# A macaron block with an RWKV mixer: the mixer's products put in a written order of twelve slots, its chunk states by a transition matrix, and w_out started beside the last group

## The chip, the cores and the metric

The kernel runs on one core of one Trainium2 chip. The metric is the device time of one execution in microseconds (us). The kernel before took 2170.04 us (median of 3 executions, 2164.2 to 2172.92). Engines are named as the profile does: PE is TensorE's matrix products, PEld its weight loads, DVE is VectorE, ACT is ScalarE, POOL is GpSimd, SP issues the DMAs of weights.

## The reference

One block on 256 rows of width 2048, float32. A vector `c` gives nine modulation vectors (`silu(c) @ w_ada + b_ada`); then three sublayers follow, each a norm, a modulation, a function, a second norm and a gated residual:

```
x = sandwich(x, ffn1)    swiglu, 2048 -> 5632 -> 2048
x = sandwich(x, mixer)   p = h @ w_in;  concat(pool(p[:512]), rwkv7(p[512:])) @ w_out
x = sandwich(x, ffn2)
```

The mixer's RWKV part has 24 heads of size 64. For every head a 64x64 state is carried over the 256 time steps:

```
state = state * w_t + (state @ -kk_t) (kk_t * a_t)^T + v_t k_t^T;   y_t = state @ r_t
```

after which each head's `y` is normed, gets a bonus `sum(r k r_k) v` and is gated by `sigmoid(xg) @ g2`. The pool part takes windowed means over time of four groups of 128 columns and multiplies each by a small matrix.

## The kernel before, in words

The kernel keeps float32 accuracy by splitting every operand of a large product into a rounded high part and a remainder (`split`, L182 on ACT makes `hi`, L183 on DVE makes `lo`), and multiplies hi·hi, hi·lo and lo·hi (`mm3`, L192 to L194; `rows_mm`, L526 to L528). Weights stream through `load` (L172) on the SP queue. The modulation vectors are no matrix products: `ada_step` loads rows of `w_ada` (L238, L241), DVE adds them up scaled by `silu(c)` (L245, L247), and small products sum over partitions (L254, L264). These steps are sprinkled over the three sublayers by counters; `ada_finish` forces what must be done by a given point.

The program is scheduled at build time: instructions are traced in the written order, which is their priority, and a scheduler with its own idea of durations fixes each engine's queue from priorities and readiness. `high_priority(n)` moves an instruction n places forward; `after` adds an edge that only fixes an order on one engine.

The mixer (`mixer`) goes in these parts:

- `outer`: the first group of w_in columns (the LoRA columns and r, k, v of the first four heads) while the normed input `hT` is made block by block.
- Six groups of four heads (two pairs of heads each, 256 columns). For each group after the first, three calls of `dense` make r, k, v (16 k-tiles, 2 column tiles and 3 products: 96 products of 128x256 each, 288 a group), and `tick` in `dense` gives out a piece of `w_ada` every third load (`ADA_MIXER = 3`).
- `stage(g, ...)` alternates two generators: `rwkv_a(g)` prepares group g, `rwkv_b(g-1)` runs the recurrence of the group before. The scheduler mixes them with the dense products.
- Then the pool columns (`dense` twice, `pool_branch`), the conversion of `y` to `hT` (L840, L841), and w_out in three column blocks (`rows_block`).

`rwkv_a`, for 4 chunks of 64 steps in each of two pairs of heads (U = 8 units of two heads): decay and gates from the LoRA products (L923, L926), their exponentials (L298); `L` (L942), the sum of squares `ns` (L944), the norm (`rsqrt`: L952, L298 twice, L309, L310, L311); `kk` (L957), `ar` (L965, L966), `kk*a` (L967), `bk` (L970 to L972); the products `G` of each chunk (L988, masked by L991); `T1` (L994); the bonus (L1003); then the inverse of a triangular 64x64 matrix per unit: 8x8 blocks on DVE (L1014 to L1030), two doublings with 32x32 products (L1054, L1062), a last one (L1075, L1082), which give `X`; the centred values `SV` (L1090) and transposes `bt` (L1097).

`rwkv_b` walks the four chunks in turn. Each chunk c > 0 needs: `ar` times the state (L1128), an addition to `rhs` on DVE (L1130), `X` times `rhs` (L1133), copies into `SV` on ACT and DVE (L1134, L1135), `bt` times `SV` plus the old state through the identity (L1144, L1141), a scaling on DVE (L1145). Then `y` (L1153, L1156), its variance (L1162), the norm (L1167, L1169), the gate (L1174) and the result (L1176).

PSUM has eight banks: two of tag `mm` for the dense products and six named `sa`, `ga`, `pb`, `zb`, `sb`, `y`. `raws` holds two weight tiles and two `ada` tiles, the split pool four pairs of `hi` and `lo`.

## Time and profile before

| what | value |
| --- | --- |
| median of 3 executions | 2170.04 us |
| the profiled execution: its own time, span of the trace | 2177.15 us, 2175.4 us |
| PE, DVE, ACT busy, share of the span | 95%, 74%, 47% |
| mean granted TensorE clock | 0.977 |
| first feed-forward sublayer | 0 to about 800 us |
| mixer, `outer` | about 805 to 876 us |
| mixer, six groups (first product of L923 to the pool products) | 876 to 1301 us |
| mixer, w_out | about 1301 to 1395 us |
| second feed-forward sublayer | 1395 us to the end |

In the rows below a busy PE is a union of records, and a record of a 128x256 product lasts 0.28 us, though the next one can start 0.12 us after it: idle time of PE is therefore what is left after the last record's whole length. A float32 product that isn't split (those of `rwkv_a` and `rwkv_b`) shows two records, a transpose one. PEclk is the granted clock as a share of full speed; in this trace it is either 1.0 or 0.5.

### The profile page before, as it was taken

What the parts mean: (1) busy time and instruction counts of PE and PEld (TensorE: products, weight loads), DVE (VectorE), ACT (ScalarE), POOL (GpSimd) and SP (SyncE); (2) the same over time, 40 slices, a digit from 0 to 9 for tenths busy, and PEclk for the clock granted to TensorE, in tenths of its full rate; (3) what the DMA queues carried; (4) which work ended last, traced back from release to release, by engine and by line L of the source; (5) the groups of instructions that cost most, each with busy time, mean ns of one, the idle gap of its engine ahead of it and who ended that gap; (6) DMA issues with size and microseconds to landing.
All of it is one profiled execution on the core that took longest, in us unless ns stands there. A gap on an engine that the chain in (4) does not pass through costs nothing.

```text
span 2175.4 us, 38002 instructions
## 1 busy us (share of the span) xinstructions
PE 2076.2 (95%) x15603; PEld 1838.6 (85%) x15603; DVE 1599.7 (74%) x2237; ACT 1016.9 (47%) x1497; POOL 0.2 (0%) x4
## 2 busy tenths in 40 slices
PE   4999999999999998989999989999999999999998
PEld 3999988888888887878887878799999888888886
DVE  6788898888887778766677565777989855555556
ACT  4534543444434465644534445653454344443443
POOL 0000000000000000000000000000000000000000
PEclk8999999999999999999999999999999999999999
DMA  9999888989888748634423315599887855555553
GB/s 324 347 317 321 280 288 314 335 308 320 312 320 297 253 127 256 179 86 139 124 67 103 102 60 194 205 346 318 280 302 266 295 193 188 182 192 194 194 184 126
DMA packets 313405, 502.37 MB, mean 231 GB/s; under 512 B 12966, under 2 KB 173839, under 8 KB 312975
## 3 DMA queue, kind: packets, MB, share of 16 engines
q1 hardware_dynamic: 311740, 496.59, 67.7%
q10 hardware_dynamic: 1490, 3.36, 0.5%
q8 instruction: 122, 2.00, 0.4%
q14 instruction: 53, 0.43, 0.1%
HBM read 497.77 MB, written 2.12 MB: 230 GB/s over the span
## 4 chain that ended last, share of the span: by engine, by line
PE 84%; DVE 8%; DMA 3%; ACT 2%; issue 2%; SPq 0%; DVEq 0%; ACTq 0%
PE mm L199 16%; PE mm L193 9%; PE mm L194 9%; PE mm L192 9%; PE mm L200 8%; PE mm L526 8%; PE mm L528 8%; PE mm L527 8%; DVE lo L183 2%; DMA ada<-in_w_ada_dram 1%; DVE acc L247 1%; DMA raw<-in_w_in_dram 1%; PE mm L254 1%; DVE G L991 1%; ACT hi L182 1%
## 5 line engine op out<-in xcount | busy, mean ns | idle before, releaser
L182 ACT CAST hi<-raw 128x1024 fp32r<-128x1024 f32 (+2 forms) x766 | 694.0, 913 | 862.8 <-PE mm L193 291.9
L183 DVE TENSOR_TENSOR lo<-raw,hi 128x1024 fp32r<-128x1024 f32 (+2 forms) x766 | 796.0, 1050 | 382.6 <-ACT hi L182 372.1
L199 PE MATMUL mm<-hT,hi 128*128 128x512 f32 x1536 | 540.1, 395 | 0.0
L192 PE MATMUL mm<-hT,hi 128*128 128x256 f32 x1824 | 525.3, 291 | 7.2 <-ACT hT L360 4.3
L193 PE MATMUL mm<-hT,hi 128*128 128x256 f32 x1824 | 527.4, 290 | 3.5 <-DVE hT L365 3.5
L194 PE MATMUL mm<-hT,lo 128*128 128x256 f32 x1824 | 525.0, 289 | 5.0 <-DVE lo L183 4.1
L200 PE MATMUL mm<-hT,lo 128*128 128x256 f32 x1536 | 431.9, 281 | 0.9 <-DVE lo L183 0.9
L247 DVE SCALAR_TENSOR_TENSOR acc<-ada,csilu,acc 128x1024 f32<-128x1024 f32 (+1 forms) x300 | 352.1, 1174 | 78.0 <-DMA ada<-in_w_ada_dram 75.4
L192 PEld LDWEIGHTS mm<-hT,hi 128*128 128x128 f32 x1824 | 353.5, 195 | 14.1 <-ACT hT L360 6.5
L193 PEld LDWEIGHTS mm<-hT,hi 128*128 128x128 f32 x1824 | 355.1, 195 | 9.4 <-DVE hT L365 5.4
L194 PEld LDWEIGHTS mm<-hT,lo 128*128 128x128 f32 x1824 | 354.3, 194 | 10.0 <-DVE lo L183 5.2
L199 PEld LDWEIGHTS mm<-hT,hi 128*128 128x128 f32 x1536 | 288.8, 188 | 67.8
L200 PEld LDWEIGHTS mm<-hT,lo 128*128 128x128 f32 x1536 | 288.0, 188 | 1.6 <-DVE lo L183 1.3
L526 PE MATMUL mm<-hi,act 128*128 128x512 f32 (+1 forms) x656 | 252.3, 385 | 0.0
L528 PE MATMUL mm<-hi,act 128*128 128x512 f32 (+1 forms) x656 | 251.9, 384 | 0.0
L527 PE MATMUL mm<-lo,act 128*128 128x512 f32 (+1 forms) x656 | 251.9, 384 | 0.0
L528 PEld LDWEIGHTS mm<-hi,act 128*128 128x128 f32 x656 | 123.3, 188 | 24.4
L526 PEld LDWEIGHTS mm<-hi,act 128*128 128x128 f32 x656 | 123.2, 188 | 24.3
L527 PEld LDWEIGHTS mm<-lo,act 128*128 128x128 f32 x656 | 123.3, 188 | 24.3
L609 DVE TENSOR_TENSOR act<-act,mm 128x512 f32<-128x512 f32 x96 | 64.2, 680 | 4.1 <-PE mm L194 3.8
L254 PE MATMUL mm<-ones,acc 128*128 128x1 f32 x128 | 20.0, 284 | 26.0 <-DVE acc L247 26.0
L254 PEld LDWEIGHTS mm<-ones,acc 128*128 128x128 f32 x128 | 20.0, 243 | 26.9 <-DVE acc L247 20.7
(382 smaller groups left out, 1794.3 us busy)
## 6 DMA issues: line engine op xcount, KB each, us to landing
raw<-in_ffn_w_down_dram SPq DMA_DIRECT2D x88, 1024.0 KB
raw<-in_ffn_w_gate_dram SPq DMA_DIRECT2D x86, 1024.0 KB
raw<-in_ffn_w_up_dram SPq DMA_DIRECT2D x86, 1024.0 KB
ada<-in_w_ada_dram SPq DMA_DIRECT2D x160, 512.0 KB
ada<-in_w_ada_dram SPq DMA_DIRECT2D x256, 256.0 KB
raw<-in_w_in_dram SPq DMA_DIRECT2D x34, 1024.0 KB
raw<-in_w_out_dram SPq DMA_DIRECT2D x16, 1024.0 KB
raw<-in_w_in_dram SPq DMA_DIRECT2D x9, 512.0 KB
```

What stands on the lines that cost most here:

```text
L182: a = nc.scalar.copy(hi, raw)
L183: d = nc.vector.tensor_tensor(lo, raw, hi.bitcast(F32), ALU.subtract)
L192: nc.tensor.matmul(ps, hi, x[:, 0, :], start=start, stop=False)
L193: nc.tensor.matmul(ps, hi, x[:, 1, :], start=False, stop=False)
L194: nc.tensor.matmul(ps, lo, x[:, 0, :], start=False, stop=stop)
L199: nc.tensor.matmul(ps.rearrange("p a t -> p (a t)"), hi, x.rearrange("p a t -> p (a t)"), start=start, stop=False)
L200: nc.tensor.matmul(ps[:, 0, :], lo, x[:, 0, :], start=False, stop=stop)
L247: self.later(nc.vector.scalar_tensor_tensor(acc, raw[:, i], ck, acc, ALU.mult, ALU.add))
L526: nc.tensor.matmul(ps, x[:, 0, ts], hi, start=start, stop=False)
L527: nc.tensor.matmul(ps, x[:, 0, ts], lo, start=False, stop=False)
L528: nc.tensor.matmul(ps, x[:, 1, ts], hi, start=False, stop=stop)
L609: nc.vector.tensor_tensor(part, part, bank, ALU.add)
```

## The change

Only the mixer's six groups, the start of w_out and the order of `w_ada` pieces change.

- **A written order on PE.** From the end of `outer` to the last recurrence, every product is tied behind the one written before it (`pe`, `mul`). A stage has 12 slots. A slot has two pieces of the next group's dense products (a piece is two k-tiles of one `dense`, 12 products), then the next segment of `b_old` (the recurrence two groups back), of `b` (one group back) and, in slots 0, 2, 4, 5, 6, 8 and 9, of `a`; after that a piece of `w_ada`. The other engines' queues are made by the scheduler as before.
- **Segments.** `rwkv_a` has seven: (0) LoRA products and exponentials, (2) `L`, `ns`, norm, `ar`, `bk`, (4) and (5) `G` of each pair, (6) transposes `bt` while DVE makes `T1` and the 8x8 blocks, (8) the product with `same` and the 8x8 inverse, (9) bonus and `SV`. `rwkv_b` has thirteen: the four 32x32 steps of the inverse, with `rhs` and the transposes `At` of `ar` beside them (0 to 3), the last doubling (4, 5), `X` times `rhs` and `X` times `At` = `Q` (6), the states of three chunks (7 to 9), `y` (10), variance and norm (11), and gate and result in slot 0 of the stage after (12).
- **One transition matrix per chunk.** `F = I + Q bt` and `E = ar + Q G` are made for all chunks at once in segment 7. Then a chunk's state is `bt SV + F S` in one PSUM tile and one scaling; the products of `ar` with the state, the addition to `rhs`, `X` times the corrected `rhs` and the identity products are gone from the walk over chunks. Per group 12 products (`ar` with the state) go, 44 come (`At` 12, `X At` 12, `Q bt` 8, `Q G` 12), and 8 are replaced one for one (`F S` for the identity).
- **Banks and tiles.** `rwkv_a` uses `sa` and `ga` alone, `rwkv_b` the other four. Some tiles lose or gain buffers, and four temporaries lie in parts of `yT` that are filled late.
- **Pool.** The pool columns are the dense pieces of the sixth stage (16 pieces, slots 0 to 7); the four `pool_branch` calls stand in its slots 8 to 11.
- **w_out.** A seventh stage holds the last recurrence, with two pieces (12 products of 128x512) of w_out's first column block per slot, taking k-tiles in the order 4 to 13, 0, 1; then 2, 3 and, last, 14 and 15, which come from the last group.
- **`w_ada`.** No pieces in `outer`; in the six stages 0.7 of a piece per slot (one load and one sum), until one more block, the third of five for the second feed-forward sublayer, is done before w_out.

```diff
-ADA_AHEAD = 1
-ADA_FFN1, ADA_MIXER, ADA_OUT, ADA_FFN2 = 2.8, 3, 3, 12
+ADA_AHEAD = ((7, 6), 2)
+ADA_FFN1, ADA_MIXER, ADA_OUT, ADA_FFN2 = 2.8, 0.7, 3, 12
+SLOTS, A_SLOTS = 12, (0, 2, 4, 5, 6, 8, 9)
...
+    def pe(self, op):
+        if self.ordered:
+            if self.pe_last is not None:
+                self.after(op, self.pe_last, "order")
+            self.pe_last = op
+        return op
+    def mul(self, ps, a, b, start=True, stop=True):
+        return self.pe(self.nc.tensor.matmul(ps, a, b, start=start, stop=stop))
...
+    def ada_run(self, upto):
+        while self.ada_pos < self.ada_end[upto]:
+            cols, k0 = self.ada_tasks[self.ada_pos]
+            width = cols[0][2]
+            per = 512 // width
+            if k0 == 0:
+                self.acc = self.tile(self.accs, [P, 2, width], tag="acc")
+            for kk in range(k0, k0 + 4, per):
+                raw = self.ada_load(cols, kk, per)
+                yield
+                self.ada_sum(raw, self.acc, kk, per)
+            self.ada_pos += 1
+            if k0 == KD - 4:
+                yield
+                self.ada_mod(cols, self.acc, self.bank("ga"))
...
     def dense(self, w, c0, n, x, cb):
...
             raw = self.load(w, 8 * kc, 8, c0, n * P)
-            self.tick()
...
                         self.mm3(ps[:, c, :], hi[:, k, cs], lo[:, k, cs], x[:, kt], kt == 0 and c == 0,
                                  kt == KD - 1 and c == n - 1)
+                yield
         for c in range(n):
             cb(c, ps[:, c, :])
...
+        for kc in order:
             raw = load(kc)
...
                         hi, lo = self.split(raw[:, pc:pc + per, 512 * h:512 * h + 512])
                         for b in (2 * h, 2 * h + 1):
                             use(b, k0, hi, lo)
+                        yield
                     continue
...
+        self.late = [self.yT[:, k:k + 2, :].rearrange("p k t -> p (k t)") for k in (0, 2, 12, 14)]
...
+        self.ordered = True
+        ada = self.ada_run(ADA_AHEAD)
+        slots = parts = 0
+        def stage(a, b, b_old, pieces, tasks):
+            nonlocal slots, parts
+            for s in range(SLOTS):
+                for _ in range(2):
+                    next(pieces, None)
+                for run, at in ((b_old, range(SLOTS)), (b, range(SLOTS)), (a, A_SLOTS)):
+                    if run and s in at:
+                        next(run, None)
+                if s in tasks:
+                    tasks[s]()
+                slots += 1
+                if a and int(slots * ADA_MIXER) > parts and (s not in A_SLOTS or s < A_SLOTS[-1]):
+                    parts += 1
+                    next(ada, None)
+        def weights(g):
+            for which in range(3):
+                self.split_ahead = 3000 if g == 1 and which < 1 else 300
+                yield from self.dense(w_in, POOL_WIDTH + which * R + g * 2 * P, 2, self.hT,
+                                      lambda i, ps: take(which, 2 * g + i, ps))
+        us = {}
+        def pool_weights():
+            for h in range(2):
+                yield from self.dense(w_in, h * 2 * P, 2, self.hT, lambda i, ps: us.__setitem__(2 * h + i, ps))
+        n = NP // 2
+        b = b_old = None
+        for g in range(n):
             state[g] = {}
-            stage(g, self.rwkv_a(state[g], g, *(rkv[g, w] for w in range(3)), lw))
-        self.pool_w = self.tile(self.w2p, [P, len(POOL_WINDOWS), P], tag="Wi", bufs=1)
-        nc.sync.dma_start(self.pool_w, I["pool_w"].rearrange("i p c -> p i c"))
-        stage(NP // 2)
-        for h in range(2):
-            self.dense(w_in, h * 2 * P, 2, self.hT, lambda i, ps: self.pool_branch(2 * h + i, ps))
-        for k in range(KD):
-            y = self.yT[:, k, :]
-            nc.scalar.copy(self.hT[:, k, 0, :], y)
-            nc.vector.tensor_tensor(self.hT[:, k, 1, :], y, self.hT[:, k, 0, :].bitcast(F32), ALU.subtract)
-        self.ada_finish((5,), self.mm)
+            a = self.rwkv_a(state[g], g, *(rkv[g, w] for w in range(3)))
+            pieces = weights(g + 1) if g < n - 1 else pool_weights()
+            tasks = {8 + i: partial(lambda i: self.pool_branch(i, us[i]), i) for i in range(4)} if g == n - 1 else {}
+            stage(a, b, b_old, pieces, tasks)
+            b, b_old = self.rwkv_b(g, state[g]), b
+            for run in (pieces, a):
+                for _ in run:
+                    pass
+        for _ in ada:
+            pass
...
+            order = [2, 3, 4, 5, 6, 0, 1, 7] if q == 0 else None
+            pieces = self.rows_pieces(load, KD, 1, lambda k: self.hT[:, k], banks, q == 3, done, more, self.mm, w, order)
+            if q == 0:
+                late(range(4, 12))
+                tasks = {1: lambda: late((12, 13)), 2: lambda: late(range(4))}
+                stage(None, b, b_old, pieces, tasks)
+                for _ in b:
+                    pass
+                late((14, 15))
+                self.ordered, self.pe_last = False, None
+            for _ in pieces:
+                pass
...
+        bt = self.tile(self.w2p, [P, U, P], tag="bt")
+        for h, tag in enumerate(("sa", "ga")):
+            ps = ch(self.bank(tag))
+            for u in range(U):
+                self.pe(nc.tensor.transpose(ps[:, u, :], pairs[h][u], self.ident[hs[h], hs[h]]))
+            nc.scalar.copy(bt[:, :, hs[h]], ps)
...
+        ps = self.bank("ga")
+        mul(ps, self.blocks, rk)
+        bv = self.tile(self.w2p, [P, 2 * T], tag="bv")
+        nc.vector.tensor_tensor(bv, ps, v, ALU.mult)
+        SV = self.tile(self.w2p, [P, U, 2, C], tag="SV")
+        ps = ch(self.bank("sa"))
+        for u in range(U):
+            for h in range(2):
+                mul(ps[hs[h], u], v[hs[h], u * C:(u + 1) * C], self.center[hs[h]])
+        for h in range(2):
+            nc.scalar.copy(SV[hs[h], :, h, :], ps[hs[h]])
+        st.update(G=G, ar=ar, bv=bv, T1=T1, Z0=Z0, Z1=Z1, SV=SV, bt=bt, wc=wc)
...
     def rwkv_b
...
+            if n == 0:
+                ps = ch(self.bank("zb"))
+                for u, h in units:
+                    mul(ps[hs[1 - h], u], G[hs[h], h, u, :C], SV[hs[h], u, h, :])
+                rhs = self.tile(self.w2p, [P, U, C], tag="rhs", bufs=1)
+                nc.scalar.copy(rhs, ps)
+            else:
+                ps = three(self.bank("y"))
+                for i, c, h in rest:
+                    mul(ps[hs[1 - h], i, c - 1], ar[hs[h], u_of(i, c), 0, :], self.ident[hs[h], hs[h]])
+                At = own("At")
+                nc.scalar.copy(At, ps)
...
+        ps, pq = ch(self.bank("pb")), three(self.bank("zb"))
         for u, h in units:
...
+            mul(ps[hs[1 - h], u], X[hs[1 - h], u], rhs[hs[1 - h], u])
+        for i, c, h in rest:
+            mul(pq[hs[1 - h], i, c - 1], X[hs[1 - h], u_of(i, c)], At[hs[1 - h], i, c - 1])
+        Q = own("Q")
+        nc.scalar.copy(SV[hs[0], :, 1, :], ps[hs[0]])
+        nc.vector.tensor_copy(SV[hs[1], :, 0, :], ps[hs[1]])
+        nc.scalar.copy(Q, pq)
         yield
...
+        E, F = own("At"), self.tile(self.w2p, [P, 2, NC - 2, C], tag="F", bufs=1)
+        for c in range(NC - 1):
+            for i, h in pairs:
+                u = u_of(i, c)
+                mul(sb[hs[h], c, i], bt[:, u, hs[h]], SV[:, u, h, :], i == 0, c == 0 and i == 1)
+            if c == 0:
+                pe, pf = three(self.bank("pb")), self.bank("zb")[:, :2 * (NC - 2) * C]
+                pf = pf.rearrange("p (i c t) -> p i c t", i=2, c=NC - 2)
+                for i, k, h in rest:
+                    q, u = hs[1 - h], u_of(i, k)
+                    if k < NC - 1:
+                        mul(pf[hs[h], i, k - 1], Q[q, i, k - 1], bt[q, u, hs[h]])
+                for i, k, h in rest:
+                    q, u = hs[1 - h], u_of(i, k)
+                    mul(pe[hs[h], i, k - 1], Q[q, i, k - 1], G[q, h, u, C:])
+                nc.vector.tensor_tensor(F, pf, self.eye.unsqueeze(1).unsqueeze(1).broadcast_to([P, 2, NC - 2, C]), ALU.add)
+            else:
+                for i, h in pairs:
+                    mul(sb[hs[h], c, i], F[hs[h], i, c - 1], S[hs[h], c - 1, i, :], False, i == 1)
+            nc.vector.tensor_tensor(S[:, c], sb[:, c], wc.rearrange("p (i c) o -> p i c o", i=2)[:, :, c, :]
+                                    .broadcast_to([P, 2, C]), ALU.mult)
+            if c == 0:
+                nc.vector.tensor_tensor(E, pe, ar.rearrange("p (i c) a t -> p i c a t", i=2)[:, :, 1:, 1, :], ALU.add)
             yield
...
         yp = self.bank("y")
         y = lambda c, i, h: half(yp, i)[hs[h], c * C:(c + 1) * C]
         for c in range(NC):
...
+            for i, h in pairs:
+                u = u_of(i, c)
+                mul(y(c, i, h), SV[:, u, h, :], G[:, h, u, C:], c == 0 and i == 0, False)
         for c in range(1, NC):
...
+            for i, h in pairs:
+                mul(y(c, i, h), S[hs[h], c - 1, i, :], E[hs[h], i, c - 1], False, c == NC - 1 and i == 1)
...
```

374 lines of the change are left out of this document (163 added, 211 removed).

## The prediction, made before the changed kernel ran

> **What bounds the kernel now.** The page comes first: the span, and PE busy for 95% of it. A busy PE says little about a single stretch, so next comes the view of busy time per engine by windows, cut at `outer` and at the first product of line 988 in each group of the mixer (the first row of groups starts at L923, the last ends with the pool). Columns: window, its length, busy us of PE, PEld, DVE, ACT, POOL, granted clock, DMA share, GB/s.
>
> ```profile
> span 2175.4 us, 38002 instructions
> PE 2076.2 (95%) x15603; PEld 1838.6 (85%) x15603; DVE 1599.7 (74%) x2237; ACT 1016.9 (47%) x1497; POOL 0.2 (0%) x4
> ```
>
> ```profile
> 805.00:875.80 70.80, 61.95 (x472) 57.06 (x471) 56.11 (x100) 44.50 (x89) 0.00 (x0) 0.98 0.83 235
> 875.80:952.00 76.20, 69.83 (x878) 61.47 (x878) 53.11 (x109) 44.18 (x83) 0.00 (x0) 0.96 0.48 140
> 952.00:1030.20 78.20, 70.23 (x936) 61.31 (x936) 56.93 (x118) 33.56 (x64) 0.00 (x0) 0.93 0.42 127
> 1030.20:1093.90 63.70, 61.49 (x892) 53.06 (x890) 45.34 (x98) 31.71 (x60) 0.00 (x0) 1.00 0.38 106
> 1093.90:1165.70 71.80, 68.59 (x918) 59.96 (x916) 46.46 (x102) 32.83 (x62) 0.00 (x0) 0.93 0.34 95
> 1165.70:1238.30 72.60, 68.61 (x912) 59.85 (x908) 46.36 (x99) 32.62 (x62) 0.00 (x0) 0.91 0.31 92
> 1238.30:1301.50 63.20, 56.07 (x855) 45.56 (x851) 47.33 (x127) 25.21 (x56) 0.00 (x0) 0.95 0.24 72
> ```
>
> The six groups take 425.7 us. PE is idle for 30.9 of them (length less busy, row by row), and the clock column costs 23.2 more (0.04 x 76.2 + 0.07 x 78.2 + 0.07 x 71.8 + 0.09 x 72.6 + 0.05 x 63.2). The one group at full clock takes 63.7 us, its neighbours 71.8 to 78.2. So PE's own work is most of each group, and the change can win from idle time and clock alone. The view of waits on PE in the same stretch says what ended the idle time (columns: us in total, times, longest), and two more windows show what follows one of these waits:
>
> ```profile
> PE ga L988 <- DVE bk L972: 3.0, 4, 0.8
> PE sa L886 <- DVE G L884: 2.9, 1, 2.9
> PE zb L1062 <- issue: 2.8, 2, 2.6
> PE sa L1003 <- DVE G L991: 2.6, 5, 0.8
> PE y L1117 <- issue: 2.0, 1, 2.0
> PE pb L1075 <- issue: 2.0, 2, 1.7
> ```
>
> ```profile
> 1121.00:1124.40 3.40, 2.50 (x48) 2.05 (x48) 1.93 (x4) 1.21 (x3) 0.00 (x0) 1.00 0.03 6
> 1124.40:1134.70 10.30, 10.30 (x53) 9.96 (x52) 1.65 (x5) 2.55 (x5) 0.00 (x0) 0.50 0.08 13
> ```
>
> No wait is long; some 45 are spread over the stretch, and since a 0.28 us record hides the first 0.16 of each, they cost about 7 us beyond the idle time. The largest kind is "issue": PE waits for nothing shown, in the middle of runs of 32x32 products. Idle time of 0.9 us in a window of 3.4 is enough to be followed by 10.3 us at half clock.
>
> The Trainium skill ("TensorE: Matmul & The Clock Gate", section "Why this matters for your kernels") asks only that idle gaps stay below about 3 us for the clock to hold. By it, no gap that I expect below would cost clock and the forecast would be 2140 us. The two rows differ from it: 0.9 us did.
>
> **The change, part by part.** Credit: all of the idle time, hidden waits and clock loss of the six groups, 30.9 + 7 + 23.2 = 61.1 us; then every loss of the new order is counted afresh. The prices of products are in the timeline of PE (start, length, records):
>
> ```profile
> 967.46 0.92 PE L1156 MATMUL y<-ar,S 64*64 64x64 f32 x24
> 972.77 0.75 PE L1062 MATMUL zb<-pm,Z 32*32 32x32 f32 x64
> 1088.19 0.28 PE L192 MATMUL mm<-hT,hi 128*128 128x256 f32 x1
> 1091.03 0.28 PE L192 MATMUL mm<-hT,hi 128*128 128x256 f32 x1
> 1093.67 0.45 PE L1128 MATMUL sb<-S,ar 64*64 64x64 f32 x8 [0.35 <-DVE S L1145]
> 1094.88 0.37 PE L988 MATMUL ga<-ar,bk 64*128 64x128 f32 x1 [0.75 <-DVE bk L972]
> ```
>
> *Products.* A 64x64 product costs 0.077 us in a long run (0.92 us for 12) and 0.11 in a burst of four (0.45). Per group 44 come in long runs (3.4 us) and the 12 of L1128 go (1.4): +2.0 us, 12 us for six groups. Bounds 2.0 to 4.0 each; I take the low end, since all four new kinds stand in runs of 8 or 12. The transposes, masks and copies that only move cost PE nothing new.
>
> *The walk over chunks.* Three hand-offs per chunk become one, with at least the slot's dense pieces between: 24 products at 0.118 us (24 starts from 1088.19 to 1091.03), 2.84 us. A link there is one or two DVE or ACT operations, so it fits; this was already hidden by dense products before and is no gain by itself.
>
> *`issue`.* The 32x32 runs now stand a slot apart. Their waits are in the credit; nothing is charged for them.
>
> *The wait that comes.* Segment 2 of `rwkv_a` (slot 2) ends with `ns`; segment 4 (slot 4) needs `ar` and `bk`. The chain of DVE and ACT between, in the timeline of the fourth group:
>
> ```profile
> 1083.78 0.69 DVE L952 TENSOR_SCALAR t<-ga 128x512 f32<-128x512 f32 x1 [0.84 <-PE ga L944]
> 1084.57 0.61 ACT L298 ACTIVATE t<-t 128x512 f32<-128x512 f32 x1
> 1085.58 0.62 ACT L298 ACTIVATE t<-t 128x512 f32<-128x512 f32 x1
> 1087.51 0.63 ACT L309 ACTIVATE t<-t 128x512 f32<-128x512 f32 x1
> 1088.17 0.69 DVE L310 SCALAR_TENSOR_TENSOR t<-t,t 128x512 f32<-128x512 f32 x1 [0.23 <-ACT t L309]
> 1089.38 0.68 DVE L311 SCALAR_TENSOR_TENSOR t<-t,t 128x512 f32<-128x512 f32 x1
> 1090.42 0.88 DVE L957 SCALAR_TENSOR_TENSOR kk<-k,cols,t 128x256 f32<-128x256 f32 x2
> 1091.62 0.69 DVE L965 TENSOR_TENSOR ar<-kk,W 128x512 f32<-128x512 f32 x1
> 1092.62 0.68 DVE L967 TENSOR_TENSOR kk<-kk,bk 128x512 f32<-128x512 f32 x1
> 1093.54 0.68 DVE L970 TENSOR_TENSOR bk<-t,Wi 128x512 f32<-128x512 f32 x1
> 1094.14 0.68 DVE L972 SCALAR_TENSOR_TENSOR bk<-kk,Wi 128x512 f32<-128x512 f32 x1
> ```
>
> It took 11.0 us here, among other work, and PE still waited 0.75 (the last row of the fence before). Its own operations sum to 7.5 us; hand-offs of 0.03 to 0.10 add some 0.3. The dense pieces need their `lo` before anything else: each 0.69 us (row below), and I count two that don't fit into the chain's ACT part: 9.2 us. The cover is two slots of dense products (5.7), segments 3 and 4 of `rwkv_b` (0.75, and about 0.7 for a half as long run) and four changes between kinds, 0.1 each by estimate: 7.5. PE then stands at the head of its queue for 1.7 us, with segment 5, the next dense pieces and the rest of the stage behind it. Six times that is 10.2, and 1.5 more in the first stage, which has no `rwkv_b` for cover: 11.7. Bounds: 0 (no `lo` in the way) to 4.3 each (two more `lo` and a sum of `w_ada`).
>
> *Other heads of the queue.* The bonus and `SV` waits (L1003 <- G, 0.5 each now) get a slot of their own; the small ones that stay are taken as 0.5 per stage, 3.
>
> *Clock.* I let four of the six waits bring one half-clock window of 3.4 us, 1.7 us lost each: 6.8. Bounds 0 and 31 (six windows of 10.3).
>
> *Pool.* Slots 8 to 11 of the sixth stage have no dense pieces left, and each ends in a pool product behind its own DVE chain. One such wait is 2.9 us today (L886). Between 2.9 and 11.6 for four I take 5, as the first two can be prepared early.
>
> *w_out beside the last group.* The same products in another order. The end of that recurrence, before k-tiles 14 and 15, is charged 2.5, near the same row.
>
> *`w_ada`.* `outer` loses its sums, the second feed-forward sublayer a block of 16; both go to the stages:
>
> ```profile
> L183 DVE TENSOR_TENSOR lo<-raw,hi 128x512 fp32r<-128x512 f32 x140 | 94.7, 687 | 61.9 <-ACT hi L182 54.0 <-ACT Z L1064 4.2 <-PE mm L194 2.4
> L247 DVE SCALAR_TENSOR_TENSOR acc<-ada,csilu,acc 128x1024 f32<-128x1024 f32 x8 | 10.2, 1276 | 0.1
> L247 DVE SCALAR_TENSOR_TENSOR acc<-ada,csilu,acc 128x512 f32<-128x512 f32 x11 | 8.2, 747 | 1.5 <-DMA ada<-in_w_ada_dram 1.4
> ```
>
> ```profile
> ACT hi L182 <- DMA raw<-in_w_in_dram: 20.7, 11, 3.6
> 1535.00:1596.00 61.00, 60.22 (x509) 59.56 (x507) 51.74 (x58) 25.09 (x29) 0.00 (x0) 1.00 0.85 295
> ```
>
> In `outer`, PE idles 8.85 us (70.80 less 61.95) and ACT waits 20.7 us for w_in, whose DMAs share the queue with `w_ada`: gain 0 to 8.9, I take 5, since two weight buffers still bound the rest. The later sublayer's stage that loses its pieces has 0.8 us of idle time: gain 0.5; in its two stages before, the pieces stay as many. The price is DVE: 295.5 us busy in the six groups (69%) plus 18.4 plus 16 x 1.28 makes 334 of some 409 (82%). The nearest row is `outer`, 79% busy with PE idle for 12.5%, against 7.3% in the groups: at most 5.2% of 409, 21 us. I charge 3, because the `lo` go first and the sums last.
>
> *Sum.* -61.1 + 11.7 + 3 + 6.8 + 5 + 12 + 2.5 + 3 - 5 - 0.5 = -22.6 us on the profiled execution's own 2177.15: 2154.5. That execution lies 7.1 above the median of 2170.04, so for the median: **2147 us**.
>
> **Rivals.**
>
> *The slots cover everything (about 2122 us).* The chain of segment 2 fits, the clock never falls, `outer` loses all its idle time: -61.1 + 3 + 5 + 12 + 2.5 - 8.9 - 0.8 = -48.3. For it: the one group at full clock, 63.7 us. Against it: 7.5 us of operations with no room for one `lo`.
>
> *VectorE takes over (about 2165).* At 82% its queue, not the slots, sets the pace: 21 instead of 3 us. For it: the `outer` row. Against: there part of the idle time belongs to the DMAs.
>
> *Slower: the head of the queue in slot 4 (about 2186).* PE can't pass a waiting product by another that is ready, which the scheduler's mix did when it put dense products into the 11 us of that chain. If each of six stages waits 4.3 us (25.8) and each wait is followed by 10.3 us at half clock (31), the sum is 38 worse. It is slower than before from about 8.7 us of wait and clock per stage. For it: the pair of windows above, 0.9 us of idle time and then 10.3 us at half clock. Against: dense products now stand in every 3.4 us.
>
> **How the numbers follow.** The forecast (2130 to 2165 as its own range) gets 0.50, the full cover 0.15, VectorE 0.17, slower 0.18. Half a percent, 2159.2 and 2180.9, is about what a measurement can tell from no change. Of the forecast 0.43 lies below 2159 and 0.07 above; with the full cover and a little of VectorE's case faster has 0.59, no change 0.23, slower 0.18. The range of 2118 to 2184 leaves out the best of the second case and half of the last.
>
> **What would show it.** Right: stages of 64 to 69 us; `issue` waits in the groups under 2 us together; about 1.7 us of idle time before the first product of `G` in each stage; half-clock windows of some 14 us in all; DVE over 80% busy. Wrong: idle time of 4 us or more there, a clock column below 0.95 in most stages, or PE waiting for `lo` (VectorE as the bound); or `outer` as long as now.

## The result, and the profile after

The changed kernel takes 2196.96 us (median of 4 executions, 2191.02 to 2199.37) where the kernel before takes 2168.49 beside it: a ratio of 1.0127, 95% interval 1.0097 to 1.0157. It is 1.3% slower; 2147 us, 1% faster, was forecast.

The profiled execution has a span of 2194.3 us (before: 2175.4). The first feed-forward sublayer is the same in both (799.7 us), and what stands behind the mixer got 3.2 us shorter (784.3 to 781.1 us), so the loss is the mixer's. That first sublayer, which no kernel here changes, takes 794.4 to 802.6 us in the traces of this document: a few us in a single trace mean little. The first view is busy time by windows: `outer`, then each group from its first low-rank product (the prediction cut at the first product of `G`, so only the sums compare), then the last group beside w_out.

```profile
805.00:881.00 76.00, 65.86 (x488) 61.57 (x487) 59.36 (x102) 49.61 (x98) 0.00 (x0) 0.96 0.79 237
881.00:937.70 56.70, 49.46 (x489) 45.58 (x487) 40.52 (x80) 29.34 (x55) 0.00 (x0) 0.94 0.50 146
937.70:1005.30 67.60, 64.08 (x979) 57.23 (x977) 43.48 (x93) 34.03 (x63) 0.00 (x0) 0.97 0.37 108
1005.30:1082.00 76.70, 66.21 (x980) 59.76 (x976) 55.63 (x114) 33.60 (x63) 0.00 (x0) 0.93 0.49 144
1082.00:1160.90 78.90, 67.17 (x980) 60.62 (x976) 61.66 (x109) 33.49 (x63) 0.00 (x0) 0.91 0.57 173
1160.90:1230.10 69.20, 64.92 (x973) 58.41 (x969) 47.43 (x100) 33.79 (x63) 0.00 (x0) 0.95 0.35 105
1230.10:1305.00 74.90, 60.83 (x783) 51.35 (x782) 48.36 (x126) 32.02 (x66) 0.00 (x0) 0.84 0.24 76
1305.00:1417.00 112.00, 110.30 (x1017) 88.06 (x1016) 68.61 (x150) 56.10 (x120) 0.00 (x0) 1.00 0.38 126
```

The six stages still take 424.0 us, though the last recurrence has left them. PE is idle for 51.3 of them (30.9 before), and the clock column costs 33 us (23.2 before). The last row is clean: 1.7 us of idle time, full clock. What PE waits for in 881 to 1417 us stands in the view of waits (us in total, times, longest):

```profile
PE ga L201 <- DVE bk L1060: 16.9, 4, 5.9
PE sa L201 <- DVE xt L1117: 13.8, 3, 7.3
PE ga L201 <- DVE mod L307: 8.9, 2, 4.5
PE sa L201 <- DVE bk L973: 3.3, 1, 3.3
PE sa L201 <- issue: 3.1, 1, 3.1
PE mm L201 <- ACT hT L919: 1.7, 1, 1.7
PE sa L201 <- ACT t L1270: 1.3, 1, 1.3
...
PE sa L201 <- ACT SV L1141: 1.1, 1, 1.1
```

Some 45 short waits have become a dozen long ones, at the heads of three segments. The first and third rows are the first `G` product of each of the six stages (5.9, 2.3, 4.5, 4.5, 4.3 and 4.4 us, 25.8 together; the page has the same sum in the idle column of `ga<-ar,bk`). In the two stages of the third row the last thing waited for was `mod`, which reads the sums of w_ada out of the same bank `ga`; it ended 0.5 us behind `bk`. The second row is `SV` behind the 8x8 inverse. The other rows of `sa` are pool products in the sixth stage.

For the comparisons below the mixer is cut in three, from the warm-up products at the end of the first feed-forward sublayer to those at the start of the second: up to the first low-rank product of stage 1, stages 1 to 5, and the rest. Before:

```profile
799.70:875.80 76.10, 66.96 (x485) 59.16 (x484) 60.59 (x118) 47.59 (x100) 0.00 (x0) 0.98 0.78 221
875.80:1223.80 348.00, 324.59 (x4377) 284.24 (x4375) 239.16 (x503) 164.23 (x311) 0.00 (x0) 0.94 0.40 114
1223.80:1391.10 167.30, 158.92 (x1413) 130.50 (x1412) 110.86 (x260) 84.44 (x176) 0.00 (x0) 0.97 0.38 122
```

After:

```profile
799.70:881.00 81.30, 70.87 (x501) 63.67 (x500) 63.85 (x120) 52.70 (x109) 0.00 (x0) 0.96 0.75 223
881.00:1230.10 349.10, 311.84 (x4385) 281.61 (x4383) 248.73 (x493) 164.25 (x307) 0.00 (x0) 0.94 0.46 136
1230.10:1413.20 183.10, 167.33 (x1790) 137.73 (x1789) 113.73 (x261) 86.06 (x177) 0.00 (x0) 0.93 0.33 108
```

The middle is as long as before (349.1 against 348.0): there the gain is missing. The 22 us of loss stand in the two ends, 5.2 and 15.8, though the first is in part a matter of the cut: the last product of `outer` ends at 875.2 us in the changed kernel (before: 876.0), and then come a wait of 2.3 us and 24 dense products of the first stage, which stand ahead of the first low-rank product. So there are two questions: what ate the gain, and what the ends lose.

### The profile page after: what moved, and what is told of

Read it like the earlier page. It is cut to its first block, busy times and chain, and to the rows that moved or that the text cites. A ratio compares the mean times of both kernels' runs of the same rounds, so it can differ in the third digit from the quotient of the medians.

```text
span 2194.3 us, 38747 instructions
## 1 busy us (share of the span) xinstructions
PE 2071.3 (94%) x15987; PEld 1843.3 (84%) x15987; DVE 1599.1 (73%) x2213; ACT 1024.0 (47%) x1503; POOL 0.2 (0%) x4
## 4 chain that ended last, share of the span: by engine, by line
PE 82%; DVE 9%; DMA 5%; ACT 2%; issue 2%; SPq 0%; DVEq 0%; ACTq 0%
PE mm L201 48%; PE mm L212 16%; PE mm L213 8%; DVE lo L186 2%; PE sa L201 2%; DVE acc L255 2%; DMA ada<-in_w_ada_dram 2%; PE ga L201 2%; DMA raw<-in_w_in_dram 2%; PE zb L201 1%; PE sb L201 1%; PE pb L201 1%; PE y L201 1%; ACT hi L185 1%; DMA raw<-in_ffn_w_gate_dram 1%
## 5 line engine op out<-in xcount | busy, mean ns | idle before, releaser
L186 DVE TENSOR_TENSOR lo<-raw,hi 128x1024 fp32r<-128x1024 f32 (+2 forms) x766 | 799.7, 1051 | 430.9 <-ACT hi L185 428.9
L201 PE MATMUL mm<-hT,hi 128*128 128x256 f32 x3648 | 685.7, 290 | 13.8 <-ACT hi L185 4.8
L201 PEld LDWEIGHTS mm<-hT,hi 128*128 128x128 f32 x3648 | 578.6, 195 | 31.3 <-issue 7.3
L255 DVE SCALAR_TENSOR_TENSOR acc<-ada,csilu,acc 128x1024 f32<-128x1024 f32 (+1 forms) x300 | 352.5, 1175 | 72.9 <-DMA ada<-in_w_ada_dram 70.1
L201 PE MATMUL mm<-hi,act 128*128 128x512 f32 (+1 forms) x1312 | 398.6, 384 | 0.0
L212 PEld LDWEIGHTS mm<-hT,hi 128*128 128x128 f32 x1536 | 288.8, 188 | 67.9
L201 PE MATMUL ga<-ar,bk 64*128 64x128 f32 x96 | 19.0, 349 | 25.8 <-DVE bk L1060 16.9
L201 PE MATMUL mm<-hi,work 128*128 128x512 f32 x128 | 40.8, 389 | 0.0
L201 PE MATMUL mm<-ones,acc 128*128 128x1 f32 x96 | 13.9, 273 | 26.2 <-DVE acc L255 26.2
L201 PEld LDWEIGHTS ga<-ar,bk 64*128 64x128 f32 x96 | 15.5, 237 | 26.8 <-DVE bk L1060 15.0
L201 PEld LDWEIGHTS mm<-ones,acc 128*128 128x128 f32 x96 | 13.7, 226 | 27.0 <-DVE acc L255 21.7
L653 ACT COPY act<-mm 128x512 f32<-128x512 f32 x32 | 18.8, 586 | 34.4 <-PE mm L201 34.4
```

Of the source, the lines that this page charges most:

```text
L186: d = nc.vector.tensor_tensor(lo, raw, hi.bitcast(F32), ALU.subtract)
L201: return self.pe(self.nc.tensor.matmul(ps, a, b, start=start, stop=stop))
L212: nc.tensor.matmul(ps.rearrange("p a t -> p (a t)"), hi, x.rearrange("p a t -> p (a t)"), start=start, stop=False)
L255: self.later(nc.vector.scalar_tensor_tensor(acc, raw[:, i], ck, acc, ALU.mult, ALU.add))
L653: nc.scalar.copy(part, bank)
```

## The experiments

All edits are to the changed kernel. Each ratio is to the kernel before on the same chip, beside it; the changed kernel's is 1.0127, from the first comparison alone. The parts are the three stretches of the mixer in the profiled execution, idle is PE's over the whole mixer.

| kernel | median us | ratio (95% interval) | parts of the mixer, us | idle us |
| --- | --- | --- | --- | --- |
| before | | 1 | 76.1 + 348.0 + 167.3 | 40.9 |
| after | 2196.96 | 1.0127 (1.0097 to 1.0157) | 81.3 + 349.1 + 183.1 | 63.5 |
| g_later | 2178.73 | 1.0085 (1.0055 to 1.0115) | whole: 601.9 | 55.2 |
| sv_later | 2182.98 | 1.0074 (1.0043 to 1.0105) | whole: 601.2 | 54.8 |
| ada_fewer | 2178.95 | 1.0073 (1.0043 to 1.0104) | whole: 595.9 | 55.0 |
| free_order | 2147.74 | 0.9932 (0.9908 to 0.9956) | 75.8 + 322.9 + 165.1 | 23.3 |
| dense_free | 2151.43 | 0.9945 (0.9923 to 0.9968) | 74.6 + 324.6 + 175.3 | 33.0 |
| free_no_late | 2144.67 | 0.9899 (0.9866 to 0.9931) | whole: 568.1 | 23.4 |
| ns_early | 2161.51 | 0.9987 (0.9972 to 1.0002) | 80.0 + 322.0 + 176.2 | 42.3 |
| free_ns | 2131.12 | 0.9849 (0.9809 to 0.9889) | whole: 549.7 | 18.4 |
| ns_sv | 2153.48 | 0.9937 (0.9918 to 0.9956) | 81.6 + 308.2 + 179.0 | 32.6 |
| dense_ns_sv | 2143.68 | 0.9902 (0.9883 to 0.9920) | whole: 561.4 | 26.4 |
| free_ns_sv | 2134.56 | 0.9855 (0.9830 to 0.9879) | 74.8 + 312.3 + 163.5 | 17.1 |
| free_ns_ada | 2126.98 | 0.9812 (0.9790 to 0.9833) | whole: 543.9 | 16.3 |
| after_ends_free | 2172.57 | 1.0040 (1.0017 to 1.0063) | 75.7 + 352.1 + 165.1 | 45.0 |
| tail_free | 2134.87 | 0.9860 (0.9831 to 0.9889) | 80.7 + 306.1 + 164.8 | 21.1 |
| ends_free | 2132.71 | 0.9841 (0.9806 to 0.9876) | 74.6 + 308.7 + 164.8 | 17.2 |
| ends_free_ada | 2121.55 | 0.9794 (0.9767 to 0.9822) | 76.4 + 304.4 + 162.0 | 15.6 |

The theory at the start: PE stands at the head of its written queue until VectorE ends the chain in front of `G`. The rivals: VectorE's queue as a whole is the bound; the 32 added products are the loss.

### Moving one head, or taking work from VectorE

`g_later`, the first `G` product one slot later:

```diff
-SLOTS, A_SLOTS = 12, (0, 2, 4, 5, 6, 8, 9)
+SLOTS, A_SLOTS = 12, (0, 2, 5, 6, 7, 9, 10)
```

> The products of G and the three segments behind them stand one slot later (slots 5, 6, 7, 9, 10 in place of 4, 5, 6, 8, 9). Theory (head of the queue): the six waits ahead of the first G product, 25.8 us after the change, lose the 3.4 us that one more slot covers, and some 6 us of them stay; of the about 20 us that the half-clock windows behind them cost, half goes. The six stages get some 30 us shorter, the time falls from 2197 to about 2167 us (2160 to 2180). Rival 1 (VectorE's queue is the bound): the chain ends later as well, or its wait comes back at the SV products, and the time stays within 5 us of 2197. Rival 2 (the 32 added products per group are the loss): PE is as busy as before, and what idle time goes is no more than 10 us of the time: 2187 or more.

The ratio fell by 0.4% (9 us), with overlapping intervals, and the mixer by 11.6 us, where the theory said some 30. (The median lies in the theory's 2160 to 2180 us, but beside a kernel before of 2163.31 us, 5 us faster than in the first comparison.) Of the waits at `G` 3.8 us are left, in the first stage, and another came in their place:

```profile
PE zb L201 <- DVE pm L1211: 16.9, 5, 4.1
PE sa L201 <- DVE xt L1117: 9.3, 4, 3.5
```

`pm` is a copy of 0.43 us that the last doubling of the recurrence needs in the same slot. The timeline of that stage shows why it is late (start, length, engine):

```profile
1096.19 0.68 DVE L1060 TENSOR_TENSOR bk<-t,y 128x512 f32<-128x512 f32 x1
1096.79 0.47 DVE L1068 SCALAR_TENSOR_TENSOR t<-r,cols,t 128x256 f32<-128x256 f32 x1
...
1097.66 0.69 DVE L1202 TENSOR_TENSOR X<-Z,consts 128x512 f32<-128x512 f32 x1
1098.38 0.43 DVE L1211 COPY pm<-pb 32x256 f32<-32x256 f32 x1
...
1098.96 0.77 PE L201 MATMUL zb<-Z,pm 32*32 32x32 f32 x21 [3.95 <-DVE pm L1211]
```

The chain of `a` holds VectorE's queue, and the recurrence's own small steps stand behind it. The first theory was too narrow: moving the product that waits helps little, since the next one that needs VectorE waits in its place (16.9 us in five stages). Rival 1 had said that the wait would come back, though at `SV` and with less gained.

`sv_later`, only the last segment moved, from slot 9 to 11:

```diff
+SLOTS, A_SLOTS = 12, (0, 2, 4, 5, 6, 8, 11)
```

> Only the last segment (bonus and SV products) is moved, from slot 9 to slot 11, three slots behind the product whose bank the 8x8 inverse reads. Theory (heads of the queue): the three waits of SV on the inverse, 13.8 us, go, with the two half-clock windows of 6.8 us behind them (6.8 us lost): 15 to 20 us faster, about 2179 us; the G waits stay at 25 us. Rival (VectorE's queue is the bound): the inverse itself ends so late in the stages with w_ada sums that the wait turns up at the next stage's first products (zb from G and SV, pb from T and Z), and the time stays within 5 us of 2197.

The waits on `xt` are gone, the `G` waits stay at 27.2 us (18.3 + 8.9), and the mixer is 12.3 us shorter; the ratio is 0.5% lower, with overlapping intervals, less than the theory's 15 to 20 us. The pool's waits grew: two on `bk L973`, 7.1 us. In the next stage 0.4 us came back.

`ada_fewer`, the extra block of w_ada back in the second feed-forward sublayer:

```diff
-ADA_AHEAD = ((7, 6), 2)
+ADA_AHEAD = ((7, 6), 1)
```

> The block of w_ada that the change drew from the second feed-forward sublayer into the stages (16 sums of 1.28 us) goes back. Theory (heads of the queue in a fixed order): the chain of segment 2 keeps its length, so the G waits stay above 3.5 us each where no sum stood in the chain; of the SV waits of 5.2 and 7.3 us up to 9 go; the feed-forward sublayer loses its 3 us again. The time falls by 3 to 10 us, to about 2190. Rival 1 (VectorE's queue is the bound): with 20 us of 334 gone from VectorE, the G waits fall to 2 us each and SV's vanish: about 2165 us.

The `G` waits did not move (16.7 + 8.9 us): the chain is not longer for these sums. Those of `SV` fell from 13.8 to 6.5. The mixer is 17.6 us shorter, 8.5 of it idle time, and the sublayer gives 1.8 back. By the ratios it is 0.5%, some 12 us, with overlapping intervals: just above the theory's 3 to 10 us and far from the rival's 30.

### Who sets the order

`free_order`, everything as changed, but no written order on PE:

```diff
-        self.ordered = True
+        self.ordered = False
```

> The new products, segments and slots are traced as before, but PE's products carry no written order: the scheduler places them by its own estimate. Theory (the written order is the loss, the new algebra costs only its 12 us of products): PE idles in the six stages for some 30 us as in the kernel before, in many waits below 1 us, with issue waits among them, none of 4 us ahead of G; about 2175 us (2165 to 2185). Rival 2 (the algebra itself is the loss, with its added products and its longer work on VectorE): no better than the written order, 2190 us or more.

0.7% faster than before and 2% faster than the changed kernel, more than the theory had hoped for. The three stretches of its mixer, to be held against those above:

```profile
794.40:870.20 75.80, 66.47 (x476) 59.31 (x475) 59.53 (x114) 47.79 (x101) 0.00 (x0) 0.98 0.73 217
870.20:1193.10 322.90, 311.92 (x4408) 280.31 (x4406) 250.96 (x500) 168.01 (x315) 0.00 (x0) 0.98 0.51 152
1193.10:1358.20 165.10, 162.15 (x1791) 133.34 (x1788) 112.25 (x261) 85.23 (x177) 0.00 (x0) 0.98 0.37 120
```

The same products, 11.0 us idle in stages 1 to 5 instead of 37.3, and the clock at 0.98. So rival 2 falls: with the added products and all else but the order, the kernel is faster than before, and the written order is the loss. How much of that gain comes from the transition matrix, and how much from the segments, the banks or the order of w_ada, no run here separates.

`dense_free`, only `mm3`'s products (the dense ones of w_in) leave the order:

```diff
-        self.mul(ps, hi, x[:, 0, :], start, False)
+        nc.tensor.matmul(ps, hi, x[:, 0, :], start=start, stop=False)
...
```

> Written order kept for the recurrences, the w_ada sums, the pool products and w_out; the dense products of w_in alone leave it, so that the scheduler may put them where PE would wait. Theory (what costs is that PE cannot pass a waiting product by a dense one that is ready): nearly all that the free order gains, 2145 to 2160 us. Rival (the order among the recurrences' own products costs as well, or the last group beside w_out): 2165 to 2185 us.

Most of the gain: in stages 1 to 5 it is level with the free order (324.6 against 322.9). What costs there is that, in the written order, PE cannot pass a waiting product by a dense one that is ready. The rest of the mixer stays 10 us longer (175.3 against 165.1): pool products and w_out are still ordered.

`free_no_late`, free order, and the late products of w_out undone:

```diff
-            order = [2, 3, 4, 5, 6, 0, 1, 7] if q == 0 else None
...
-                stage(None, b, b_old, pieces, tasks)
+                stage(None, b, b_old, iter(()), tasks)
```

> No written order, and the late products of w_out undone: the last recurrence is traced alone, and w_out's products behind it in the order of their k-tiles. Theory (beside the last group w_out fills PE in the hand-offs of a walk over three chunks): 8 to 20 us slower than the free order at 2148, that is 2156 to 2168 us. Rival (the scheduler moves w_out's products up beside the recurrence by itself): within 4 us of 2148.

No loss: the intervals overlap with those of the free order (0.9866 to 0.9931 and 0.9908 to 0.9956). The scheduler brings w_out's products up by itself (in this trace they stand between those of the last recurrence from 1250 us on); writing them there gains nothing that can be measured.

### Shortening the chain

`ns_early`, written order, with `ns`, its inverse root and `kk` in a segment of their own in slot 1 (they need only `k`), and eight slots (0, 1, 2, 4, 5, 6, 8, 9):

```diff
-        L, ns = self.bank("sa"), self.bank("ga")
...
+        ns = self.bank("ga")
+        mul(ns, self.blocks, sq)
+        n2 = t1()
+        nc.vector.tensor_scalar(n2, ns, 1e-24, None, ALU.max)
+        self.rsqrt(nrm, None, n2, sq, None, None)
...
+        yield
+
+        L = self.bank("sa")
```

> Written order kept. The product ns, its inverse root and kk get a segment of their own in slot 1 (ns needs only k), so that of the chain between slot 2 and the first G product only W, Wi, the two ar, kk times a and the bk are left: some 4.5 us shorter in operations. With one slot more for G the wait had only gone over to zb <- pm in the same slot, 16.9 us in all, pm being queued on VectorE behind the chain. Theory A (the chain's length sets the wait): the waits of 4.3 us at G fall below 1.5 us each without coming back at pm, idle time of the six stages from 51 to some 30 us, 30 to 40 us faster than the changed kernel with the clock: about 2155 us where the changed kernel would stand at 2191 beside a before of 2163. Theory B (VectorE's queue is behind by a backlog of lo, shifts and sums, whatever the chain): G or pm still waits 3 us or more per stage, and the time stays within 8 us of 2191.

```profile
PE sa L201 <- DVE xt L1120: 13.9, 3, 7.8
PE ga L201 <- DVE bk L1063: 3.6, 1, 3.6
```

One `G` wait is left, that of the first stage, and `pm` does not wait: 27 us less in stages 1 to 5, 1.4% of the time. This is theory A, 6 us short of its number. VectorE's busy time is the same (423.26 us in the mixer, 426.31 after the change), so it was not the amount of VectorE's work but the point at which the chain could start.

`free_ns`, the same without the written order:

> No written order, and ns in slot 1 as in the run beside it. Theory (with a free order the chain lies behind dense products but for 4.2 us ahead of two G products): up to 8 us faster than the free order alone at 2148: 2140 to 2148 us. Rival (the chain bounds the stage whatever the order): idle time falls by more than that and the clock with it: below 2138 us.

14 us of the mixer (563.8 to 549.7), as the rival had it: with a free order the long chain had cost too.

`ns_sv`, written order, both heads moved:

```diff
+SLOTS, A_SLOTS = 12, (0, 1, 2, 4, 5, 6, 8, 11)
```

> Written order, ns in a segment of its own in slot 1, and SV in slot 11 in place of 9: both heads that waited are moved. Theory (two mis-timed heads of the queue explain the loss): the 13.9 us that SV still waited in the run with ns alone go, with 6 us of clock behind them, and do not come back: about 2145 us (2138 to 2150) where ns alone took 2161.5; idle time of the six stages near 17 us. Rival (a fixed order always finds the next head that waits): the idle time goes over to other products and the time stays above 2154 us.

`dense_ns_sv`, the same with the dense products free, and `free_ns_sv`, the same with no order at all:

> Only the dense products of w_in are free; the written order is kept for the rest, with ns in slot 1 and SV in slot 11. Theory (once no head waits long, the order among the recurrences' own products costs nothing but the pool's 8.7 us): 2136 to 2142 us, within 8 us of the run with the full written order and both moves. Rival (the order among them still costs): 2145 us or more.

> No written order, ns in slot 1, SV traced in slot 11. Theory: the two SV waits of 4.6 us that are left with the free order go, 3 to 7 us: 2124 to 2128 us beside 2131 for the free order with ns alone. Rival (a wait that PE can fill costs nothing, and a later SV only holds up the recurrence of the next stage): 2131 us or up to 6 more.

`ns_sv` came out between its two numbers. The stretches say why. Of `ns_sv`:

```profile
802.40:884.00 81.60, 71.08 (x500) 63.63 (x499) 64.65 (x122) 53.36 (x110) 0.00 (x0) 0.96 0.75 226
884.00:1192.20 308.20, 299.77 (x4384) 270.29 (x4382) 245.02 (x494) 163.08 (x305) 0.00 (x0) 0.99 0.52 153
1192.20:1371.20 179.00, 165.37 (x1792) 136.23 (x1789) 112.30 (x259) 85.89 (x177) 0.00 (x0) 0.93 0.34 110
```

In stages 1 to 5 the written order is now as short as the free one (308.2 against 312.3), 41 us less than after the change; the ends are as bad as ever. With a free order the later `SV` is worth nothing (0.9855 against 0.9849): a wait that PE can fill costs nothing that shows. The guess for `dense_ns_sv` was 2136 to 2142 us, its rival's 2145 or more; it took 2143.68.

`free_ns_ada`, free order, early `ns`, w_ada as in `ada_fewer`:

> No written order, ns in slot 1, and the block of w_ada back in the second feed-forward sublayer. Rival V (VectorE, 304 of 382 us busy in the six stages, is now what sets the pace): 20 us less of its work there make the stages some 8 to 15 us shorter, less 3 us in the feed-forward sublayer: 2120 to 2126 us. Theory (with a free order VectorE's work lies beside PE's): the stages gain what SV still waits, up to 5 us, the feed-forward sublayer loses 3: 2128 to 2133 us.

The mixer is 5.8 us shorter than in `free_ns`, the ratio lower by 0.4% with overlapping intervals: the time lies between the two guesses, and these executions do not settle which is right.

### The ends

The order is written for a part of the stages only; the line below is that of `after_ends_free` (the changed kernel's slots) and of `ends_free` and `ends_free_ada` (those of `ns_sv`), and in `tail_free` it reads `g < n - 1`:

```diff
         for g in range(n):
             state[g] = {}
+            self.ordered = 0 < g < n - 1
```

> The changed kernel with its own slots and segments; only the written order is taken from the first and the sixth stage and from w_out. Theory: the waits at G and SV of stages 2 to 5 stay (15.5 and 12.5 us), those of the first and the sixth stage and the pool (5.9 + 1.3 + 4.4 + 8.7 us) go, with their clock: 20 to 28 us faster than the changed kernel, which stands at 2193 beside a before of 2166: about 2169 us. Rival (the ends cost little by themselves): above 2180 us.

> ns in slot 1, SV in slot 11; the written order ends before the sixth stage, so that the pool's products and the last group beside w_out are placed by the scheduler. Theory (the rest of the loss lies at the ends, most of it where pool products stand at the head behind their VectorE chains): 10 to 15 us faster than 2153, about 2140 us; no pool wait above 1 us. Rival (the loss is spread over the stages): 2148 us or more.

> As the run beside it, and the written order starts with the second stage only. Theory (in the first stage the fixed order puts the low-rank products and the first G behind w_in's transfers and a chain that no recurrence covers): 4 to 8 us faster than that run, about 2134 us, level with the free order (2131 to 2135). Rival (the first stage is bounded by its transfers): no faster than that run.

> As ends_free, and the block of w_ada back in the second feed-forward sublayer. Theory (with no head that waits, VectorE's work lies beside PE's; as with the free order, where it brought 2131 to 2127): 2 to 6 us faster than ends_free, about 2130 us. Rival: the sublayer loses as much as the stages gain, and the time is that of ends_free.

With the changed kernel's own slots, freeing both ends takes 18 us from the last stretch (183.1 to 165.1) and 2.6 from the first two together (430.4 to 427.8). The middle keeps its waits (352.1): `SV` 12.6, `G` 17.2 us. By the ratios the two ends are worth 0.9%, 19 us, just under the 20 to 28 of the forecast. With both heads moved, the end is worth 14.2 us (179.0 to 164.8; by the ratios 0.8%, and the intervals do not overlap) and the start 3.5 (386.8 to 383.3; the intervals overlap, so that it is worth anything is not shown). The row of 81 us for the first stretch overstates the start, because of the 24 dense products (x501 against x476).

`ends_free_ada` beats both kernels: 2121.55 us, 0.9794 of before. Of `ends_free_ada`:

```profile
797.30:873.70 76.40, 67.73 (x476) 60.65 (x475) 59.84 (x114) 47.99 (x101) 0.00 (x0) 0.96 0.73 216
873.70:1178.10 304.40, 301.37 (x4408) 271.82 (x4406) 231.99 (x486) 169.19 (x315) 0.00 (x0) 1.00 0.46 134
1178.10:1340.10 162.00, 158.11 (x1775) 129.29 (x1772) 110.91 (x257) 86.03 (x177) 0.00 (x0) 0.99 0.38 122
```

Five stages of 60.9 us at full clock, 3 us idle: the forecast of 64 to 69 us per stage was within reach of this algebra, with other slots (`ends_free`, with all of its w_ada, has 61.7). Against `ends_free` its median is 11 us lower, with overlapping intervals; in the traces 5.3 us of that are the mixer's and 4.9 the first sublayer's, which the edit does not touch.

## Why the prediction was wrong

For the mixer the prediction had 22.1 us less, and 22.1 us more came: 44 us missed. The rows of the three stretches split them (the clock by its column, as in the prediction):

| part of the mixer's time | forecast, us | measured, us |
| --- | --- | --- |
| idle time of PE | -10.7 (30.9 of credit and 5 of `outer`, less 25.2 of new waits) | +22.6 |
| clock | -16.4 | +9.6 |
| the rest, PE's work at full clock | +5 (12 of products less 7 of hidden waits) | -10.1 |

So idle time was 33 us too low and the clock 26, while PE's own work was priced some 15 us too dear. (Idle time inside half-clock windows stands in both of the first two rows, so the last is a few us less wrong than it looks.) The idle part has its names: against the terms of the sum, the `G` waits were 14 us too low, the other heads 11, `outer` 6 and the pool 4. Of what the prediction named as signs of being wrong, three came: 4 us or more ahead of `G`, a clock column below 0.95 in four of six stages, and `outer` as long as before. PE waiting for `lo` did not.

**The wait at slot 4: the term that failed first.** The prediction put 1.7 us per stage (9.2 of chain less 7.5 of cover); it was 4.3 on average, 25.8 us in all. In the fourth stage the timeline of VectorE from the end of `ns` to the first `G` product reads, with the PE rows at its two ends and in its middle (other rows left out):

```profile
1093.40 1.02 PE L201 MATMUL ga<-y,consts 128*128 128x512 f32 x2
1094.23 0.69 DVE L1062 TENSOR_TENSOR ar<-r,W 128x512 f32<-128x512 f32 x1 [1.68 <-ACT W L338]
1094.84 0.68 DVE L1045 TENSOR_SCALAR t<-ga 128x512 f32<-128x512 f32 x1
...
1096.73 0.69 DVE L186 TENSOR_TENSOR lo<-raw,hi 128x512 fp32r<-128x512 f32 x1 [1.13 <-ACT hi L185]
...
1098.54 0.48 DVE L778 SCALAR_TENSOR_TENSOR r<-mm,cols,r 128x255 f32<-128x255 f32 x1
1098.93 0.68 DVE L186 TENSOR_TENSOR lo<-raw,hi 128x512 fp32r<-128x512 f32 x1
...
1101.02 0.69 DVE L186 TENSOR_TENSOR lo<-raw,hi 128x512 fp32r<-128x512 f32 x1 [0.38 <-ACT hi L185]
...
1101.80 0.69 PE L201 MATMUL pb<-Z,T 32*32 32x32 f32 x32
1102.44 0.69 DVE L186 TENSOR_TENSOR lo<-raw,hi 128x512 fp32r<-128x512 f32 x1
...
1104.65 0.48 DVE L1068 SCALAR_TENSOR_TENSOR t<-r,cols,t 128x256 f32<-128x256 f32 x1
...
1105.65 0.68 DVE L1060 TENSOR_TENSOR bk<-t,y 128x512 f32<-128x512 f32 x1
...
1106.95 0.55 PE L201 MATMUL ga<-ar,bk 64*128 64x128 f32 x1 [4.46 <-DVE mod L307]
```

From the end of `ns` (1094.42) to the first `G` product at 1106.95 are 12.5 us. The cover, to the end of the last product before it (1102.49), is 8.1: that half was right. In the chain were four `lo`, not two, two shifts of r, k, v (L778, one shown), two operations for `rk` (L1068, one shown), which nothing needs before slot 9, and `ar` from r (L1062) ahead of its start. The two `lo`, two shifts and two `rk` that were not counted take 2 x 0.69 + 2 x 0.48 + 2 x 0.48 = 3.3 us, which is the 12.5 less the 9.2 that were. The prediction counted the operations of the chain and left out of its sum what the same segment and the dense pieces bring to the same queue. Its upper bound, 4.3 each, was the truth, to the digit by luck: the two more `lo` were there, but shifts and `rk` in place of the sum of w_ada. The row of 11.0 us in the trace of before, quoted there, was the better estimate than the sum made from it.

**Other heads, 3 us.** Wrong by 11: `SV` has a slot of its own but stands one slot behind the product whose bank the 8x8 inverse reads, some fifteen VectorE operations in a row. In the stages with the most w_ada it waited 5.2 and 7.3 us.

**Clock, 6.8 us.** The column costs 33 us in the six stages. Within each of the ten waits of 2.3 us or more (six ahead of `G`, two of `SV`, two of the pool), or up to 1.4 us behind it, 3.4 to 13.7 us at half clock begin, much as the upper bound (31) had it. The sum let four short windows come, against its own row of 10.3 us behind 0.9 us of idle time. Part of the waits lies inside these windows, so the two sums overlap.

**Pool, 5 us.** Four waits of 3.3, 3.1, 1.3 and 1.1 us, 8.8, and the clock at 0.84 in that stage. Freeing all that is ordered from there on was worth 18 us, about what that stretch lost against before (15.8).

**`outer`, -5 us.** It did not come: idle time up to the first low-rank product is 10.4 us, 9.1 before. What is written later is not executed later here: the scheduler moved the w_ada loads and sums up again, and VectorE makes the same 19 sums of L255 in `outer` as it did before at L247 (first at 816.5, last at 875.4 us). The text on the change, no pieces in `outer`, tells what is written, not what runs.

**VectorE, 3 us.** Moving the block costs 0.54, 0.37 and 0.47% in three pairs (the first with the waits of the written order), each with overlapping intervals, about 8 to 12 us; in the traces the mixer gets 17.6, 5.8 and 5.3 us shorter. So 3 was too low, within the bounds of 0 to 21. VectorE at over 80% was wrong after the change (248.73 of 349.1 us, 71%), only because the stages stayed long; `ends_free` has 249.88 of 308.70 (81%), with 6.5 us of PE idle. Here high VectorE use does not set the pace; where its operations stand does.

**Products, +12, and the credit, -61.1.** The products were not measured by themselves. In the table above PE's work did not grow; for `free_order` the same reckoning gives 6 us more, about the 5 that were counted. So their price hangs on the order, and why it does stays open. The three `issue` waits shown in the prediction, 6.8 us, are gone, as said, and most of the credit can be had: the middle is 39.3 us shorter in `ends_free` than before and 43.6 in `ends_free_ada`, products included. **w_out, 2.5:** 1.7 measured, right; that writing it late gains nothing was not foreseen. **Second sublayer, -0.5:** -3.2.

**The rivals.** The slower one, with a chance of 0.18, had the place, the 4.3 us (25.8 in all) and the clock (31 against 33); the time went past its 2186 by `SV`, the pool and `outer`, which that rival did not have. Its argument against, dense products in every slot, does not help a queue that stands. Full cover (2122 us) is what `ends_free_ada` reaches (2121.55; 2125 by its ratio), but by a chain that starts earlier and an order that is written for four stages only.

## What to carry to other kernels

A written order on an engine turns every late operand into idle time of all that is queued behind it: before fixing it, list for each head of the queue everything that its producer's queue holds in that time, other segments' work included, and start the chain earlier (`ns_early`, 1.4% of the time) rather than moving the consumer (`g_later`, 0.4%). Where the slots are right, a fixed order is as good as the scheduler's; where work is irregular, as in the last stages here (14 to 18 us), leave it free. When a trace holds the whole chain, take its measured length, not a sum of its parts.

## What the runs showed of the hardware

Short idle times were followed by half clock. Of the changed kernel, two windows in a row:

```profile
958.90:962.40 3.50, 1.16 (x14) 1.00 (x15) 3.47 (x8) 0.98 (x2) 0.00 (x0) 1.00 0.52 184
962.40:965.80 3.40, 3.40 (x20) 3.18 (x17) 2.20 (x5) 0.00 (x0) 0.00 (x0) 0.50 0.02 5
```

2.3 us without a product, then 3.4 us at half clock with PE busy throughout. The Trainium skill ("TensorE: Matmul & The Clock Gate", section "Why this matters for your kernels") asks for no gaps above about 3 us; this gap was shorter, and half clock followed.

More surprising, of `ends_free`:

```profile
1206.60:1210.00 3.40, 3.35 (x30) 3.15 (x29) 1.30 (x4) 0.42 (x2) 0.00 (x0) 1.00 0.18 72
1210.00:1216.90 6.90, 6.90 (x68) 6.39 (x67) 5.00 (x10) 2.51 (x6) 0.00 (x0) 0.51 0.31 90
```

Here PE was busy for 3.35 of 3.40 us, and half clock followed all the same. 16 of the 30 products in that window are those of one column that sum w_ada over partitions:

```profile
L201 PE MATMUL ga<-ones,acc 128*128 128x1 f32 x16 | 1.9, 251 | 0.0
```

This burst of 16 (1.95 us) stands in ten of the traces with at most 0.05 us of idle time around it. In seven of them half clock begins in it or within 2.3 us of its end; in `free_ns`, `g_later` and `dense_ns_sv` none follows. Two other bursts, of 8 (1.05 us), stand as tightly in nine of these ten, and none of the 18 is followed by half clock. That such narrow products do not keep the clock, if enough of them fall into one stretch, is a guess from these counts; no run isolates it.
